# Two MoE expert layouts: narrow column chunks in eleven weight buffers, and rows up to 11 KB in eight

## The chip, the cores and the metric

The kernel runs on one core of a Trainium2 chip. The metric is the device time of one execution in microseconds (us), the median of several runs. The core has five engines: TensorE (PE, matrix products), VectorE (DVE), ScalarE (ACT), GpSimd (POOL), and SyncE (SP), which here issues the transfers of weights from device memory to the on-chip buffer. PE sums into eight accumulator banks.

## The reference, cut to what matters

Two layers of a hybrid block (attention, state space, differential attention) on 256 latent and 256 context tokens of width 1024. The second layer ends with eight SwiGLU experts, of which each latent token uses two:

```python
def _swiglu(h, w_gu, w_down):
    g, u = jnp.split(h @ w_gu, 2, axis=-1)
    return (jax.nn.silu(g) * u) @ w_down

def _moe(h, w_r, b_r, we_gu, we_down):
    ...
    for e in range(N_EXP):
        y = y + gates[..., e:e + 1] * _swiglu(h, we_gu[e], we_down[e])
    return y
```

All is float32. An expert's `w_gu` is 1024 x 5632 (gate columns, then up columns, 2816 each), its `w_down` 2816 x 1024; all eight together are 277 MB, and every one is read once.

## The kernel before

The experts (function `moe`) are the last 700 us or so of the program. The experts are sorted by their number of tokens. Five are computed as **large** ones (`expert`, room for 128 tokens), three as **small** ones (room for 32). The order of the parts is g0, 1, d0, 2, g6, 3, d6, 4, g7, 5, d7: a number alone is a large expert, g a small expert's gate and up (`small_gate_up`), d its down (`small_down`).

*Weight buffers.* `raw_tile` hands out the buffers of a ring in turn, from pools that MRB gives: (5, 1, 5), eleven buffers of 8 KB per partition (1 MB each). SP issues one transfer per buffer, in the order of use, as soon as the buffer's last reader is done. Six of the eleven are free early, before the router has run.

*Large experts.* Tokens are the fixed operand, weights stream through PE. The gate and up columns go in three chunks of 1024, 1024 and 768. For each chunk come the gate's eight steps of 128 rows (two steps per transfer), then the up's eight. In each step (`product`) the weights are split into two parts for full precision: ACT copies a rounded part `mwh` (L1348), DVE subtracts to get the rest `mwl` (L1349; `msplit`, MSB = 4 buffers of each). PE multiplies the tokens' two parts with `mwh` (L1369) and, one step later, the main part with `mwl` (L1358, the correction). After the gate's steps ACT applies silu into `msl` (L1448), after the up's steps DVE multiplies (L1450), PE transposes in blocks of 128 columns (L1455), and ACT and DVE split the transposed block (`mah`, `mal`). Down has 22 steps over the 2816 rows, two per transfer, in the same three passes. The gate's sums lie in two of the three banks S, the up's in the two banks mm, the down's in y and one S.

*Small experts.* 32 tokens fill only a quarter of PE's columns, so four matmuls run in four column groups: two halves of the output columns times two rows of the reduction. Nothing is split; a float32 matmul stands in the profile as two records. Gate and up go in two chunks, 2 x 1024 and 2 x 384 columns, with transfers of [128, 2, 1024] (4 KB pieces of rows) and [128, 4, 384] (1.5 KB pieces). The four partial sums are copied by ACT (L1531) and folded and transposed on PE (`fold`, L1538). The small down has eleven steps, each of one transfer that holds both halves' 128 rows.

*Between the parts* the steps call a generator that gathers the next expert's tokens (transposes and products on PE, copies on ACT and DVE), and each expert's result is scattered into the output rows a little into the next part (`scatter_now`). The order of the instructions on an engine is set when the program is built, by a scheduler that works from the order of the code, and the engine executes them in that order.

Of the kernel before, what the change touches and what calls it, by code (L numbers as in the profile page):

```python
# [12 lines left out]
F = mybir.dt.float32  # L13
# [18 lines left out]
FT = 22  # L32
NE = 8
# [9 lines left out]
XB, START, MRB, MSB = 1, 1, (5, 1, 5), 4  # L43
# [71 lines left out]
def kernel(ctx: ExitStack, tc: tile.TileContext, I, out: bass.AP):  # L115
# [1130 lines left out]
    def moe(L, pp, late, mraw):  # L1246
# [51 lines left out]
        big = mw.tile([128, 6, NE, NE], F, name="big")  # L1298
# [80 lines left out]
        def gather(rk, res, small=False):  # L1379
# [21 lines left out]
            for c in range(2):  # L1401
# [6 lines left out]
                xg = mw.tile([128, 512], F, name="xg", tag="msl", bufs=2)  # L1408
# [19 lines left out]
        def expert(X, gt, gu_src, dn_src, side=()):  # L1428
# [4 lines left out]
            for o, w in ((0, 1024), (1024, 1024), (2048, 768)):  # L1433
                sl = mw.tile([128, 1024], F, name="msl", tag="msl", bufs=2)
                halves = [(c, min(512, w - c)) for c in range(0, w, 512)]
                for a, tag in enumerate(("S", "mm")):
                    pg = [p_(tag, "m" + "gu"[a]) for _ in halves]
                    for kp in range(4):
                        raw = raw_tile([128, 2, w])
                        SP.dma_start(raw, gu_src(kp, a, o, w))  # L1440
# [3 lines left out]
                        if o == 0 and a == 0 and kp == 1:  # L1444
                            scatter_now()
                    for (c, n), p in zip(halves, pg):
                        if a == 0:
                            S.activation(sl[:, c:c + n], p[:, :n], AF.Silu)  # L1448
                        else:
                            V.tensor_tensor(sl[:, c:c + n], sl[:, c:c + n], p[:, :n], op=OP.mult)  # L1450
                for c, n in halves:
                    f = n // 128
# [3 lines left out]
                    ah = mw.tile([128, f, 128], FR, name="mah", tag=f"mah{f}", bufs=5 if f == 4 else 1)  # L1456
                    al = mw.tile([128, f, 128], FR, name="mal", tag=f"mal{f}", bufs=5 if f == 4 else 1)
                    pv = pt[:, :n].rearrange("p (f q) -> p f q", f=f)
# [355 lines left out]
```

## Time and profile before

| | |
|---|---|
| time, median of 3 runs | 1818.12 us (1816.6 to 1825.8) |
| profiled execution, its own time | 1821.04 us |
| its span, first to last instruction | 1819.2 us |
| mean granted clock of PE | 0.951 of full |
| busy share of the span: PE, DVE, ACT | 91%, 63%, 48% |
| chain of work that ended last | PE 77%, DMA 8%, DVE 7% |
| moved by DMA | 436.09 MB |

The profile is of one execution. Its page gives the busy time of each engine, 40 equal slices of the span, the chain of work that ended last, and the costliest groups of instructions; the trace behind it gives any stretch instruction by instruction. The experts stand in slices 25 to 40. In a row of the timeline, x8 is a run of eight records of one line; the end of a matmul is modelled.

### The profile page before, as it was taken

What the parts mean: (1) busy time and instruction counts of PE and PEld (TensorE: products, weight loads), DVE (VectorE), ACT (ScalarE), POOL (GpSimd) and SP (SyncE); (2) the same over time, 40 slices, a digit from 0 to 9 for tenths busy, and PEclk for the clock granted to TensorE, in tenths of its full rate; (3) what the DMA queues carried; (4) which work ended last, traced back from release to release, by engine and by line L of the source; (5) the groups of instructions that cost most, each with busy time, mean ns of one, the idle gap of its engine ahead of it and who ended that gap; (6) DMA issues with size and microseconds to landing.
All of it is one profiled execution on the core that took longest, in us unless ns stands there. A gap on an engine that the chain in (4) does not pass through costs nothing.

```text
span 1819.2 us, 26372 instructions
## 1 busy us (share of the span) xinstructions
PE 1663.7 (91%) x9454; PEld 1244.2 (68%) x9454; DVE 1154.5 (63%) x2224; ACT 874.4 (48%) x1447; POOL 321.9 (18%) x254
## 2 busy tenths in 40 slices
PE   5898989887999999987999984899999999999995
PEld 2677657674988888876786672487686685784782
DVE  4673668658632343288587756288785586982895
ACT  3433545543622132335444652376673574772770
POOL 1221013334420022474232141000000000000000
PEclk8999998878999999999899996899999999999998
DMA  9327454328633233345676227999999999999995
GB/s 306 86 67 236 127 149 123 107 66 269 188 93 96 89 101 96 110 165 167 209 223 207 65 82 300 395 406 409 408 406 376 399 406 409 406 408 387 408 407 229
DMA packets 248153, 436.09 MB, mean 240 GB/s; under 512 B 15025, under 2 KB 166329, under 8 KB 248017
## 3 DMA queue, kind: packets, MB, share of 16 engines
q1 hardware_dynamic: 246096, 429.55, 66.2%
q0 software_dynamic: 1920, 4.81, 1.0%
q8 instruction: 76, 1.25, 0.3%
q14 instruction: 61, 0.49, 0.1%
HBM read 431.08 MB, written 3.23 MB: 239 GB/s over the span
## 4 chain that ended last, share of the span: by engine, by line
PE 77%; DMA 8%; DVE 7%; issue 2%; ACT 2%; POOL 0%; SPq 0%; ACTq 0%; DVEq 0%; POOLq 0%
PE mg L1369 6%; PE mu L1369 6%; PE mdn L1369 5%; PE gu L273 5%; PE gu L274 5%; PE gu L276 4%; DMA raw<-in_w_ada 4%; PE mu L1358 3%; PE mg L1358 3%; PE mdn L1358 3%; PE tok L276 2%; DMA mraw<-in_exp_w_gu 2%; PE ada L316 2%; PE tok L273 2%; PE SC L919 2%; PE tok L274 2%
## 5 line engine op out<-in xcount | busy, mean ns | idle before, releaser
L1349 DVE TENSOR_TENSOR mwl<-mraw,mwh 128x1024 fp32r<-128x1024 f32 (+1 forms) x350 | 389.4, 1160 | 37.2 <-ACT mwh L1348 20.2
L1348 ACT ACTIVATE mwh<-mraw 128x1024 fp32r<-128x1024 f32 (+1 forms) x350 | 337.8, 1013 | 61.4 <-PE mg L1369 22.9
L260 POOL TENSOR_TENSOR wlo<-raw,whi 128x1024 fp32r<-128x1024 f32 (+2 forms) x93 | 224.1, 2416 | 482.2 <-ACT whi L259 435.1
L259 ACT ACTIVATE whi<-raw 128x1024 fp32r<-128x1024 f32 (+2 forms) x168 | 168.2, 1004 | 237.3 <-PE dn L274 71.9
L260 DVE TENSOR_TENSOR wlo<-raw,whi 128x1024 fp32r<-128x1024 f32 (+2 forms) x75 | 90.5, 1206 | 144.1 <-ACT whi L259 142.8
L273 PE MATMUL gu<-HI,whi 128*128 128x512 f32 (+1 forms) x400 | 144.2, 369 | 2.3 <-ACT whi L259 2.3
L274 PE MATMUL gu<-LO,whi 128*128 128x512 f32 (+1 forms) x400 | 144.9, 369 | 0.0
L273 PE MATMUL tok<-whi,HI 128*128 128x256 f32 (+2 forms) x400 | 108.7, 301 | 5.4 <-ACT xin L550 4.3
L274 PE MATMUL tok<-whi,LO 128*128 128x256 f32 (+2 forms) x400 | 106.4, 295 | 5.2 <-DVE LO L444 5.1
L316 PE MATMUL ada<-raw,cT 128*32 128x256 f32 x768 | 75.5, 430 | 37.8 <-DMA raw<-in_w_ada 35.9
L276 PE MATMUL gu<-HI,wlo 128*128 128x512 f32 (+1 forms) x400 | 98.5, 368 | 0.0
L273 PEld LDWEIGHTS tok<-whi,HI 128*128 128x128 f32 x400 | 79.2, 199 | 14.9 <-issue 5.4
L273 PEld LDWEIGHTS gu<-HI,whi 128*128 128x128 f32 x400 | 75.7, 190 | 15.8 <-ACT whi L259 2.5
L274 PEld LDWEIGHTS tok<-whi,LO 128*128 128x128 f32 x400 | 79.3, 199 | 9.1 <-DVE LO L444 5.8
L274 PEld LDWEIGHTS gu<-LO,whi 128*128 128x128 f32 x400 | 76.1, 191 | 12.8
L276 PEld LDWEIGHTS gu<-HI,wlo 128*128 128x128 f32 x400 | 70.5, 189 | 12.9
L273 PE MATMUL dn<-whi,ah 128*128 128x512 f32 x176 | 70.3, 399 | 5.6 <-ACT whi L259 5.6
L276 PE MATMUL tok<-wlo,HI 128*128 128x256 f32 (+2 forms) x400 | 72.3, 299 | 1.9 <-DVE nw L227 1.9
L1369 PE MATMUL mg<-mwh,Xh 128*128 128x512 f32 x240 | 72.5, 383 | 1.7 <-ACT mwh L1348 1.6
L1369 PE MATMUL mdn<-mwh,mah 128*128 128x512 f32 x220 | 70.1, 400 | 0.9 <-ACT mwh L1348 0.9
L1369 PE MATMUL mg<-mwh,Xl 128*128 128x512 f32 x240 | 70.8, 376 | 0.0
L1369 PE MATMUL mu<-mwh,Xl 128*128 128x512 f32 x240 | 70.7, 376 | 0.0
(361 smaller groups left out, 3496.5 us busy)
## 6 DMA issues: line engine op xcount, KB each, us to landing
mraw<-in_exp_w_gu SPq DMA_DIRECT2D x128, 1024.0 KB, 15.8
mraw<-in_exp_w_down SPq DMA_DIRECT2D x88, 1024.0 KB, 15.6
mraw<-in_exp_w_gu SPq DMA_DIRECT2D x64, 768.0 KB, 13.8
raw<-in_w_ada SPq DMA_DIRECT2D x88, 512.0 KB, 4.8
raw<-in_ffn_w_gu SPq DMA_DIRECT2D x100, 256.0 KB, 3.4
raw<-in_w_in SPq DMA_DIRECT2D x38, 512.0 KB, 5.1
raw<-in_ffn_w_down SPq DMA_DIRECT2D x30, 512.0 KB, 3.7
E<-cscr POOLq DMA_DIRECT2D x12, 384.0 KB, 7.2
```

What stands on the lines that cost most here:

```text
L259: S.activation(hi, raw, AF.Copy)
L260: (eng or V).tensor_tensor(lo, raw, hi.bitcast(F), op=OP.subtract)
L273: T.matmul(o, ah, bh, start=start and i == 0, stop=False)
L274: T.matmul(o, *((ah, bl) if wa else (al, bh)), start=False, stop=False)
L276: T.matmul(o, *((al, bh) if wa else (ah, bl)), start=False, stop=stop and i == n - 1)
L316: T.matmul(pa[32 * j:32 * j + 32, hs], cT[:, k], w[j], start=(k == 0), stop=(k == KC - 1), tile_position=(0, 32 * j), skip_group_check=True)
L919: T.matmul(po[:, :n], qTC(t)[b0:b0 + 32, h // 2], kTC[b0:b0 + 32, h // 2, :n], start=True, stop=True)
L1348: S.activation(wh, raw, AF.Copy)
L1349: V.tensor_tensor(wl, raw, wh.bitcast(F), op=OP.subtract)
L1358: T.matmul(pc[:, :w], xh, wl[:, c * 512:c * 512 + w], start=False, stop=stop)
L1369: T.matmul(pc[:, :w], x, wh[:, c * 512:c * 512 + w], start=start and x is xh, stop=False)
```

## The change

- Ring: eleven buffers of 8 KB become eight of 11 KB (MRB = (4, 0, 4)), four of them free early.
- Large gate and up: two chunks of 1408 columns instead of three; a transfer is [128, 2, 1408], pieces of 5.5 KB of a row instead of 4 or 3 KB. Each chunk has three accumulator pieces, 512, 512 and 384: the gate's in S, S, S, the up's in mm, mm and y, the down's in y and mm.
- Small gate and up: one pass over whole rows. A transfer is [128, 2816], one whole row half of 11 KB per partition; two of them make a step.
- Down, large and small: a partition holds two neighbouring rows (8 KB in one piece) instead of two rows that lie 128 apart; the eleventh row of each half comes alone (4 KB). So partition p of a half stands for rows 11p to 11p + 10, and the transposes before down, and the small experts' folds, take every eleventh column of `msl` (`slv`, `views`).
- Split buffers: two of `mwh` and three of `mwl`, 1408 wide, instead of four and four of 1024. `msl` has one buffer of 1408 columns, and the gathered tokens and the results have a pair of buffers of their own.

In all 224 weight transfers instead of 280. The core of the diff:

```diff
-XB, START, MRB, MSB = 1, 1, (5, 1, 5), 4
+XB, START, MRB, MSB = 1, 1, (4, 0, 4), (2, 3)
...
-            wh = ms.tile([128, 1024], FR, name="mwh", tag="mwh", bufs=MSB)[:, :n]
-            wl = ms.tile([128, 1024], FR, name="mwl", tag="mwl", bufs=MSB)[:, :n]
+            wh = ms.tile([128, HW], FR, name="mwh", tag="mwh", bufs=MSB[0])[:, :n]
+            wl = ms.tile([128, HW], FR, name="mwl", tag="mwl", bufs=MSB[1])[:, :n]
...
-            for o, w in ((0, 1024), (1024, 1024), (2048, 768)):
-                sl = mw.tile([128, 1024], F, name="msl", tag="msl", bufs=2)
...
+            for c in range(2):
+                sl = mw.tile([128, HW], F, name="msl", tag="msl", bufs=1)
+                for a, tags in enumerate((("S", "S", "S"), ("mm", "mm", "y"))):
+                    pg = [p_(tag, "m" + "gu"[a]) for tag in tags]
                     for kp in range(4):
-                        raw = raw_tile([128, 2, w])
-                        SP.dma_start(raw, gu_src(kp, a, o, w))
+                        raw = raw_tile([128, 2, HW])
+                        SP.dma_start(raw, gu_src(kp, a, c))
...
+                slv = sl.rearrange("p (q j) -> p j q", j=HB)
+                for b0, f in FOURS:
                     pt = p_tp()
                     for q in range(f):
-                        T.transpose(pt[:, q * 128:(q + 1) * 128], sl[:, c + q * 128:c + (q + 1) * 128], ident)
...
+                        T.transpose(pt[:, q * 128:(q + 1) * 128], slv[:, b0 + q], ident)
...
-            pd = [p_("y", "mdn"), p_("S", "mdn")]
...
+            pd = [p_("y", "mdn"), p_("mm", "mdn")]
+            for c in range(2):
+                for j in range(0, HB, 2):
+                    if c or j:
+                        next(side, None)
+                    n = min(2, HB - j)
+                    raw = raw_tile([128, n, 1024])
+                    SP.dma_start(raw, dn_src(c, j, n))
...
+                    for j in range(2):
+                        raws.append(raw_tile([128, DFF]))
+                        SP.dma_start(raws[j], gu_src(2 * kp + j, a))
...
+                    for (o, n), p in zip(PIECES, pg):
+                        tiles4(lambda h, j, r, tp: T.matmul(
+                            p[r, :n], Xf[:, 2 * kp + j, 0:32], raws[j][:, h * HW + o:h * HW + o + n], start=kp == 0,
+                            stop=kp == 3, tile_position=tp, skip_group_check=True))
...
+            def dn(c, j, n):
+                return rows(WDf, e * DFF + c * HW, HW).rearrange("(p j) n -> p j n", j=HB)[:, j:j + n]
```

The engines' order moves at three places. In the listings a row is a line of the code, the tile written and those read, the shape, in brackets whom it waits for, and xN a repetition. The line numbers of the changed kernel are some 5 higher.

DVE in expert 1, from up to down, before (`msl<-msl,mu` is the product with up, `mal` the rest of a transposed block):

```order
1580 L1450 TENSOR_TENSOR msl<-msl,mu 128x512 [waits PE_49]
1581 L1450 TENSOR_TENSOR msl<-msl,mu 128x256 [waits PE_49]
1582 L1349 TENSOR_TENSOR mwl<-mraw,mwh 128x1024 [waits DMAHW6_49,Activation_49]
1583 L1349 TENSOR_TENSOR mwl<-mraw,mwh 128x1024 [waits Activation_49]
1584 L1460 TENSOR_TENSOR mal<-tp,mah 128x512 [waits Activation_49]
1585 L1460 TENSOR_TENSOR mal<-tp,mah 128x256 [waits Activation_49]
1586 L1349 TENSOR_TENSOR mwl<-mraw,mwh 128x1024 [waits DMAHW7_49,Activation_49]
```

The same place on DVE in the changed kernel:

```order
1564 L1354 TENSOR_TENSOR mwl<-mraw,mwh 128x1024 [waits DMAHW6_49,PE_49,Activation_49]
1565 L1454 TENSOR_TENSOR msl<-msl,mu 128x512 [waits PE_49] x2
1566 L1354 TENSOR_TENSOR mwl<-mraw,mwh 128x1024 [waits Activation_49]
1567 L1454 TENSOR_TENSOR msl<-msl,mu 128x384 [waits PE_49]
1568 L1465 TENSOR_TENSOR mal<-tp,mah 128x512 [waits Activation_49] x2
1569 L1354 TENSOR_TENSOR mwl<-mraw,mwh 128x1024 [waits DMAHW7_49,Activation_49]
1570 L1354 TENSOR_TENSOR mwl<-mraw,mwh 128x1024 [waits PE_49,Activation_49]
1571 L1465 TENSOR_TENSOR mal<-tp,mah 128x384 [waits Activation_49]
```

A split of down's second step now stands between the second and the third product, and the transposed blocks' parts follow later.

PE in g6, where the gate's steps end, before (`mg<-mraw,Xs` is a small expert's gate matmul on one column group):

```order
4898 L1413 MATMUL tp<-cf,xg 128x128 [waits Activation_49]
4899 L1413 MATMUL tp<-cf,xg 128x128 x3
4900 L1524 MATMUL mg<-mraw,Xs 32x512 [waits DMAHW4_49]
4901 L1524 MATMUL mg<-mraw,Xs 32x512 x3
4902 L1524 MATMUL mg<-mraw,Xs 32x512 [waits DMAHW5_49]
4903 L1524 MATMUL mg<-mraw,Xs 32x512 x3
4904 L1524 MATMUL mg<-mraw,Xs 32x512 [waits DMAHW6_49]
4905 L1524 MATMUL mg<-mraw,Xs 32x512 x3
```

PE at the same place of the changed kernel:

```order
4888 L1528 MATMUL mg<-mraw,Xs 32x512 [waits DMAHW7_49]
4889 L1528 MATMUL mg<-mraw,Xs 32x512 x5
4890 L1528 MATMUL mg<-mraw,Xs 32x384 x3
4891 L1528 MATMUL mg<-mraw,Xs 32x512 [waits DMAHW0_49]
4892 L1528 MATMUL mg<-mraw,Xs 32x512
4893 L1528 MATMUL mg<-mraw,Xs 32x384
4894 L1528 MATMUL mg<-mraw,Xs 32x512 [waits DMAHW1_49]
4895 L1528 MATMUL mg<-mraw,Xs 32x512 x5
4896 L1528 MATMUL mg<-mraw,Xs 32x384 x3
4897 L1540 MATMUL tp<-fold,msl 128x64 [waits Activation_49]
4898 L1540 MATMUL tp<-fold,msl 128x64 x3
```

Before, four matmuls follow each transfer, on two column groups. Now three follow the first of two transfers, all on one column group, and nine the second, on the other three; and the folds come when the gate's copies are done, before up.

PE in d0, before (`mdn<-mraw,sact` is a small down's matmul):

```order
4464 L1558 MATMUL mdn<-mraw,sact 32x512 [waits DMAHW4_49]
4465 L1558 MATMUL mdn<-mraw,sact 32x512 x3
4466 L1413 MATMUL tp<-cf,xg 128x128 [waits DVE_49,Activation_49]
4467 L1413 MATMUL tp<-cf,xg 128x128 x3
4468 L1405 MATMUL gather<-tok,Sm 128x512 x4
4469 L1558 MATMUL mdn<-mraw,sact 32x512 [waits DMAHW5_49]
4470 L1558 MATMUL mdn<-mraw,sact 32x512 x3
```

PE at the same place of the changed kernel:

```order
4451 L1564 MATMUL mdn<-mraw,sact 32x512 [waits DMAHW6_49]
4452 L1410 MATMUL gather<-tok,Sm 128x512 [waits DVE_49]
4453 L1410 MATMUL gather<-tok,Sm 128x512 x3
4454 L1418 MATMUL tp<-cf,xg 128x128 [waits Activation_49]
4455 L1418 MATMUL tp<-cf,xg 128x128 x3
4456 L1410 MATMUL gather<-tok,Sm 128x512 x4
4457 L1564 MATMUL mdn<-mraw,sact 32x512 [waits DMAHW7_49]
4458 L1564 MATMUL mdn<-mraw,sact 32x512 x6
```

Before, four matmuls follow one transfer. Now one follows the first of two transfers and seven the second.

## Rows read from the trace of the kernel before

**Rows 1.** Page, slices of the span: DMA busy tenths, GB/s.

```profile
DMA  9327454328633233345676227999999999999995
GB/s 306 86 67 236 127 149 123 107 66 269 188 93 96 89 101 96 110 165 167 209 223 207 65 82 300 395 406 409 408 406 376 399 406 409 406 408 387 408 407 229
```

**Rows 2.** Waits of PE, 1100 to 1800 us: total us, times, longest us.

```profile
PE mu L1524 <- DMA mraw<-in_exp_w_gu: 4.6, 1, 4.6
...
PE mdn L1558 <- DMA mraw<-in_exp_w_down: 1.0, 1, 1.0
```

**Rows 3.** PE's timeline, g6: start us, us, line, operation [idle before it].

```profile
1386.58 0.64 PE L1369 MATMUL mdn<-mwh,mah 128*128 128x512 f32 x2
...
1387.05 0.62 PE L1369 MATMUL mdn<-mwh,mal 128*128 128x512 f32 x2
...
1388.07 1.91 PE L1524 MATMUL mg<-mraw,Xs 128*32 128x512 f32 x8
...
1402.08 3.63 PE L1524 MATMUL mg<-mraw,Xs 128*32 128x512 f32 x24
...
1407.57 7.10 PE L1524 MATMUL mu<-mraw,Xs 128*32 128x512 f32 x64
...
1415.38 2.00 PE L1538 MATMUL tp<-fold,mal 128*128 128x64 f32 x16 [0.72 <-ACT mal L1531]
...
1423.46 3.04 PE L1524 MATMUL mu<-mraw,Xs 128*32 128x384 f32 x28
...
1427.16 0.88 PE L1538 MATMUL tp<-fold,mal 128*128 128x64 f32 x6 [0.65 <-ACT mal L1531]
...
1429.40 0.73 PE L1369 MATMUL mg<-mwh,Xh 128*128 128x512 f32 x2 [1.36 <-ACT mwh L1348]
```

**Rows 4.** SP's timeline in g6; DMA issues, page and 1385 to 1395 us (last: us to landing).

```profile
1390.02 23.84 SPq L1518 DMA_DIRECT2D mraw<-in_exp_w_gu  x13
...
mraw<-in_exp_w_gu SPq DMA_DIRECT2D x128, 1024.0 KB, 15.8
...
mraw<-in_exp_w_gu SPq DMA_DIRECT2D x3, 1024.0 KB, 5.5
```

**Rows 5.** Stretch: us, busy us by engine (records), granted clock, DMA share, GB/s.

```profile
1386.00:1392.00 6.00, 6.00 (x28) 2.45 (x26) 1.46 (x3) 0.83 (x2) 0.00 (x0) 1.00 0.97 341
```

**Rows 6.** Stretches with one row size landing: 3, 4 and 1.5 KB; same columns.

```profile
1209.00:1221.00 12.00, 12.00 (x60) 9.99 (x59) 10.86 (x12) 9.14 (x12) 0.00 (x0) 1.00 1.03 401
1230.00:1280.00 50.00, 48.28 (x234) 33.98 (x233) 37.49 (x41) 28.54 (x33) 0.00 (x0) 1.00 1.03 409
1412.00:1422.00 10.00, 9.28 (x86) 4.52 (x79) 1.33 (x4) 2.95 (x7) 0.00 (x0) 1.00 1.07 373
```

**Rows 7.** Stretch in g0, same columns.

```profile
1150.00:1156.00 6.00, 2.96 (x8) 0.56 (x8) 0.00 (x0) 0.60 (x1) 0.00 (x0) 0.68 1.06 375
```

**Rows 8.** Groups, 1170 to 1290 us, ACT and DVE: busy us, mean ns.

```profile
L1348 ACT ACTIVATE mwh<-mraw 128x1024 fp32r<-128x1024 f32 x59 | 58.9, 1062 | 9.2 <-PE mdn L1369 3.8 <-PE mg L1369 3.4 <-DMA mraw<-in_exp_w_gu 1.3
...
L1448 ACT ACTIVATE msl<-mg 128x512 f32<-128x512 f32 x5 | 2.8, 597 | 5.5 <-PE mg L1358 5.5
...
L1450 DVE TENSOR_TENSOR msl<-msl,mu 128x512 f32<-128x512 f32 x5 | 3.3, 686 | 4.0 <-PE mu L1358 4.0
```

**Rows 9.** PE's timeline, small down d0.

```profile
1266.63 1.06 PE L1558 MATMUL mdn<-mraw,sact 128*32 128x512 f32 x8
...
1280.00 5.36 PE L1558 MATMUL mdn<-mraw,sact 128*32 128x512 f32 x48
```

**Rows 10.** Timeline, expert 1 from up to down, DVE and PE.

```profile
1235.18 1.02 DVE L1450 TENSOR_TENSOR msl<-msl,mu 128x512 f32<-128x512 f32 x2 [1.81 <-PE mu L1358]
...
1236.04 0.82 PE L1455 MATMUL tp<-cf,msl 128*128 128x128 f32 x6
...
1236.12 2.35 DVE L1349 TENSOR_TENSOR mwl<-mraw,mwh 128x1024 fp32r<-128x1024 f32 x2
...
1238.55 0.73 PE L1369 MATMUL mdn<-mwh,mah 128*128 128x512 f32 x2 [0.31 <-ACT mwh L1348]
```

More of the change, by code (lines that the diff above doesn't have):

```diff
@@ L1407, in gather @@
                 yield
-                xg = mw.tile([128, 512], F, name="xg", tag="msl", bufs=2)
+                xg = mw.tile([128, 512], F, name="xg", tag="xg", bufs=2)
                 S.activation(xg, px, AF.Copy)
@@ L1465, in finish_half @@
                 Yl = mw.tile([128, 512], FR, name="Yl", tag="Yl", bufs=2)
[L1466 removed]
+                Y = mw.tile([128, 512], F, name="Y", tag="xg", bufs=2)
                 V.tensor_tensor(Y, p, g2[:, cs_], op=OP.mult)
@@ new lines, in small_gate_up @@
+            act = mw.tile([128, HB, 64], F, name="sact")
+            parts = (mw.tile([128, HW], F, name="msl", tag="msl", bufs=1),
+                     ms.tile([128, HW], F, name="mwl", tag="mwl", bufs=MSB[1]))
+            for a, tags in enumerate((("S", "S", "S"), ("mm", "mm", "y"))):
+                pg = [p_(tag, "m" + "gu"[a]) for tag in tags]
+                for kp in range(4):
+                    raws = []
+                    for j in range(2):
+                        raws.append(raw_tile([128, DFF]))
+                        SP.dma_start(raws[j], gu_src(2 * kp + j, a))
+                    if a or kp > 1:
+                        next(side, None)
+                    for (o, n), p in zip(PIECES, pg):
+                        tiles4(lambda h, j, r, tp: T.matmul(
+                            p[r, :n], Xf[:, 2 * kp + j, 0:32], raws[j][:, h * HW + o:h * HW + o + n], start=kp == 0,
+                            stop=kp == 3, tile_position=tp, skip_group_check=True))
+                    if a == 0 and kp == 1:
+                        scatter_now()
+                for (o, n), p in zip(PIECES, pg):
+                    S.activation(parts[a][:, o:o + n], p[:, :n], AF.Copy)
@@ new lines, in small_gate_up @@
+            views = [t.rearrange("p (q j) -> p j q", j=HB) for t in parts]
+            for b, f in FOURS:
+                pt = p_tp()
+                for a, t in enumerate(views):
+                    for q in range(f):
+                        T.matmul(pt[:, a * 256 + q * 64:a * 256 + (q + 1) * 64], t[:, b + q],
+                                 fold.rearrange("p h s -> p (h s)"), start=True, stop=True)
+                at = act[:, b:b + f]
+                pv = pt.rearrange("p (a f s) -> p a f s", a=2, f=4)[:, :, :f]
+                S.activation(at, pv[:, 0], AF.Silu)
+                V.tensor_tensor(at, at, pv[:, 1], op=OP.mult)
@@ L1549, in small_down @@
             ST = X[2]
[L1550 to L1552 removed]
+            pd = p_("S", "mdn")
+            for j in range(0, HB, 2):
+                if j == 2:
                     scatter_now()
[L1554 removed]
+                if j >= 4:
                     next(side, None)
[L1556 to L1560 removed]
+                    next(side, None)
+                n = min(2, HB - j)
+                raws = []
+                for h in range(2):
+                    raws.append(raw_tile([128, n, 1024]))
+                    SP.dma_start(raws[h], dn_src(h, j, n))
+                for k in range(n):
+                    tiles4(lambda c, h, r, tp: T.matmul(
+                        pd[r], act[:, j + k, 32 * h:32 * h + 32], raws[h][:, k, c * 512:(c + 1) * 512],
+                        start=j + k == 0, stop=j + k == HB - 1, tile_position=tp, skip_group_check=True))
             Y = mw.tile([128, 512], F, name="Yh", tag="Yh", bufs=2)
```

98 lines of the change are left out of this document (20 added, 78 removed).

## The prediction

> **What bounds the kernel now.** I read the page's 40 slices first, then the experts' part alone. From slice 25 on the DMA digits are 9 and the rates stand near 406 GB/s, where they were mostly under 300 earlier [rows 1]: the change works where the transfers never rest. That alone suggests a DMA bound. But the waits of PE (TensorE) between 1100 and 1800 us name a transfer as releaser for only 4.6 us in the first small expert and 1.0 us in the last small down [rows 2]. In between PE goes from work to work. The order of time in a small gate/up (expert g6, 1388.07 to 1429.40 us) shows why both look full: PE has matmuls to the end, and SP issues the last 13 pieces in 23.84 us [rows 3, 4]. So engine and queue are in balance, and the link between them is the ring of weight buffers: when expert 2 ends the rate falls to 341 GB/s [rows 5], and a piece lands 5.5 us after its issue, against 15.8 us over the whole program [rows 4]: the queue has run empty because every slot is full. A faster transfer there finds no slot. The large experts are PE's (it is 12.00 us of 12.00 busy, first of [rows 6]); only the first small expert and the last down wait for data.
>
> The page is of an execution of 1821.0 us (span 1819.2); the median of the three runs is 1818.1, 2.9 less. I sum against 1821.0 and take off 2.9 at the end. About 0.5% (9 us) is what a measurement of this kernel can tell from no change.
>
> **What the transfers save.** Stretches in which pieces of one row size land run at 373 GB/s (1.5 KB rows), 401 (3 KB) and 409 (4 KB) [rows 6]. Per row on one of 16 engines that is 65.9, 122.6 and 160.2 ns: a line of 9.3 ns plus 0.0368 ns per byte. Run on to 5.5, 8 and 11 KB (an estimate) it gives 416, 421 and 425 GB/s. A large gate/up (23.1 MB) falls from 56.7 to 55.5 us, a large down (11.5 MB, last row of each half still 4 KB) from 28.2 to 27.4, a small gate/up from 57.9 to 54.3, a small down by 0.8. That is 5 x 2.0 + 3 x 3.6 + 3 x 0.8 = 23 us of queue time, the most that the change can bring; nothing, if a row beyond 4 KB costs per byte what a 4 KB row does.
>
> How much of it arrives depends on the ring. Eleven slots of 8 KB become eight of 11 KB, 11 MB as before, but an 8 KB piece of down, or the 4 KB piece at the end of a half, also takes a whole slot. The queue's lead at the start of a small gate/up is then 8 x 3.39 = 27.1 us of transfer.
>
> *First small expert (g0).* Its data arrive late: PE waits 4.6 us, the granted clock falls to 0.68 of full, between 2.4 and 1.2 GHz [rows 2, 7]. 3.6 us less transfer, and the last pair of pieces now brings three wide matmuls per column group after it lands: I take -3 (-6 to +2).
>
> *g6 and g7.* Data side: first slots come back 2.4 us in, the queue restarts in some 2 us, the eight remaining pieces take 27.1 and land by 34 to 36 us; one last set of matmuls (2.4), copies (1.8) and 14 folds with a gather (2.9) end at 41 to 43, where before 41.3 passed. PE's side: before, five halves of a step stand alone at 1.91 us (x8), then 3.63, 7.10 and for the 384 columns four runs of 6.9 us together (one of them stands there): 27.2 [rows 3]. From x8, a matmul of 512 columns is 0.92 us on its column group, so one of 384 is 0.69, and a set of three pieces takes 2.4 us. By the new order the gate stands in four lone sets and a run of two, the up in four sets: 10 x 2.4 = 24 us, 3 less. The copies before the folds can't be used piece by piece any more, since a fold takes every eleventh column: 2 waits of 1.7 to 1.9 us for three copies (0.6 us each, [rows 8]) instead of 0.72, 0.65 and 1.36 [rows 3]: +1. Both sides end near 41 to 43: +1 each (-3 to +4).
>
> Those sets rest on a matmul of one column group not blocking the others. The x64 row shows it: the order has four matmuls on groups 0 and 1 before four on 2 and 3, yet 64 records take 7.10 us, eight pairs' worth only if all four groups run together [rows 3]. The Trainium skill ("TensorE: Matmul & The Clock Gate", The mechanism) says that matmuls start and end strictly in the order of the program. By that rule the x64 row would be near 14 us and three matmuls on group 0 would hold up the other nine for 1.84 us. The trace disagrees at the depth of four records on a group that it shows; six in a row, as now, it doesn't show.
>
> *Small downs.* Two pieces now stand for two steps, and the scheduler puts one lone matmul before the second piece and seven behind. Before, five lone steps of 1.06 us and a run of six of 5.36 [rows 9], 10.3 us. Now three lone matmuls (0.98), three groups of seven (two rounds, 1.86) and a run of 5 steps (4.4): 12.9. d0 and d6 +2.6 each (0 to +4); d7 +1.6, as its 1.0 us wait for data goes.
>
> **Large experts: two buffers of split weights instead of four.** A step of 1408 columns is nine matmuls; two of 512 are issued each 0.47 us [rows 3], so 6 x 0.23 + 3 x 0.175 = 1.92 us, and all steps together cost what they did. The split on ACT takes 1.06 us per 1024 columns, so about 1.4 for 1408 [rows 8], and can start when PE is done with the six main matmuls of the step before last. It is ready 1.5 us later; PE needs it after a correction (0.64), the next main pass (1.28) and its correction, 2.56 us later: 1 us of cover, in down 0.7 (1.2 against 0.47 + 0.93 + 0.47). That cover is gone wherever ACT has something else first. Behind the gate three silus (1.7 us) stand before the third split of up: 0.2 us of wait, twice.
>
> The main place is the change from up to down. Before, PE's first product of down uses banks that are long free, and then two transposed blocks that need only the last two products; PE is idle for 0.31 us [rows 10]. Now down's two sums take banks that up has just filled, so the first matmul waits for the first product on DVE (0.69, [rows 8]). The transposes read every eleventh column, so they need all three products, and the order puts a split of 1.2 us (two in 2.35, [rows 10]) before the third: 0.69 + 0.69 + 1.22 + 0.5 = 3.1 us, from which the rest of up's correction and five matmuls of down (1.6 us) are taken: 1.5 to 1.6 us idle in two waits. Then the third split of down stands behind two copies of the transposed blocks (0.6 each): 0.5 us. In sum 2.1 + 0.4 - 0.3 = +2.2; I take 1.8, as a part of the silus' wait is hidden: 5 x 1.8 = +9 (0.5 to 3 each).
>
> The 22 transposes of an expert load weights with a stride of eleven elements; no row of before has a strided weight load. The nearest row is a transpose as it is, six in 0.82 us [rows 10]. Bounds: 0, since the load runs beside other matmuls, and one more transpose of 0.12 us each: 2.7 us per expert, 21 us in all eight. I take 0, the value of those rows.
>
> **Sum:** -3 + 2 x 1 + 2 x 2.6 + 1.6 + 9 = +14.8: 1836 against the profiled execution, 1833 against the median.
>
> **The rivals.**
> (1) *The transfers decide everywhere.* For it: the DMA digits of 9. Against it: the rows on a full ring, and PE's missing waits. If PE's busy time hides waiting, the queue's 23 us arrive, less 2 to 3 for the coarser ends: -20, 1798. Chance 0.12.
> (2) *Gains and losses cancel.* If the scheduler's order meets the chip better than I think, with 0.5 us per large expert, nothing at the small downs and -3 at g0, the sum is about 0 to +2: 1818 to 1820. It decides if the waits at up to down fall below 0.7 us. Chance 0.26.
> (3) *Strided weight loads cost.* At 0.06 to 0.12 us for each of 22 in eight experts, +11 to +21 on my sum: 1844 to 1854. The Trainium skill ("SBUF — State Buffer", Door 1: The DMA port swizzle) says that accesses which leave a 16-byte line each time pay, and allows a stride of 4 fp32 free; here it is 11. No run here shows it yet. Chance 0.13.
> (4) *A column group's three matmuls block the others.* A pair of pieces then costs 3.4 instead of 2.4 us; with six such pairs in g6 and g7 that is +6 each, 1845; g0 hides it behind its data. It decides if six records queued on one group stop the next group's first. Chance 0.09. By the rule of the Trainium skill weighed above ("TensorE: Matmul & The Clock Gate", The mechanism) it would come out so.
> (5) *Rows over 4 KB bring nothing*: g0's gain is gone, g6 and g7 end 3 us later: +9, 1842. Chance 0.06.
> My forecast of 1833 (1825 to 1840) has 0.34.
>
> **How the numbers follow.** Slower by over 0.5% (above 1827): my case without its lowest part 0.31, and rivals 3 to 5 with 0.28: 0.59. Within 0.5%: rival 2 and that lowest part, 0.29. Faster: rival 1, 0.12. For 8 in 10 I leave out most of rival 1 and the upper end of rival 3: 1813 to 1852.
>
> **What would show it.** In the changed profile: landings of gate/up pieces every 3.4 us where the queue is full, rates of 415 to 425 GB/s there, and more stretches below 380 at the ends of large experts, since the ring fills sooner. PE's waits should name DVE's product (msl) and ACT's split (mwh) at up to down, about 2 us per large expert, and a wait of some 1.8 us for the copies before folds. The large experts should grow by about 2 us each, the small downs by 2 to 3. I am wrong if those parts shrink (rival 1), if transposes take visibly more than 0.14 us each (rival 3), or if up's four steps in g6 take 14 instead of 10 us (rival 4).

## The result, and the profile after

The changed kernel takes 1870.12 us, median of four runs (1866.5 to 1875.6); the kernel before took 1821.47 beside it. The ratio is 1.027, with a 95% interval of 1.0228 to 1.0313: slower by 49 us, and beyond the upper end of the predicted range (1852). The profiled execution took 1872.4 us (span 1870.7), mean granted clock 0.947.

I compare by parts, from a part's first matmul to that of the next. In the profile after, g0 begins 6.3 us earlier (1120.1 against 1126.4 us); in all the profiles below it begins between 1117 and 1132, and I leave that aside. Each small part is taken with the large expert behind it, because the scheduler lets neighbours overlap by a few matmuls. Lengths in us, of one profile each; the ratios are of medians against the kernel before on the same chip. A part's first matmul doesn't cut the work at the same place in every kernel, as the last matmuls of the large expert before can follow it: at g6 2 records in the kernel before and in b4_ring8, 14 in the changed kernel, e2_folds, e9_olddown, b3_split23 and b5_both, 20 in e5_oldsmall. Two records take 0.47 us, so up to 4 us stand one column further right. At d7 they are 20 in the changed kernel and 2 before: some 4 of the 6.5 us by which d7 grows.

| kernel | g0+1 | d0+2 | g6+3 | d6+4 | g7+5 | d7 | ratio (95%) |
|---|---|---|---|---|---|---|---|
| before | 140.3 | 121.4 | 136.2 | 121.1 | 135.9 | 38.0 | 1 |
| after | 145.6 | 129.3 | 152.6 | 125.7 | 152.8 | 44.5 | 1.027 (1.0228 to 1.0313) |
| e1_order | 146.0 | 128.0 | 155.8 | 129.6 | 149.7 | 42.4 | 1.0343 (1.0318 to 1.0367) |
| e2_folds | 142.3 | 127.5 | 146.7 | 124.2 | 146.4 | 40.7 | 1.0188 (1.0166 to 1.021) |
| e7_rows | 142.8 | 126.6 | 145.2 | 123.2 | 145.2 | 38.8 | 1.0144 (1.0107 to 1.0181) |
| e4_order_folds | 143.1 | 127.1 | 146.2 | 127.5 | 147.2 | 41.0 | 1.0203 (1.0163 to 1.0243) |
| e5_oldsmall | 145.9 | 120.3 | 151.5 | 120.6 | 153.5 | 40.1 | 1.0241 (1.0223 to 1.0259) |
| e9_olddown | 147.8 | 119.5 | 152.6 | 119.9 | 152.4 | 36.6 | 1.0203 (1.0168 to 1.0239) |
| b5_both | 145.0 | 118.5 | 148.2 | 117.1 | 148.9 | 37.8 | 1.0113 (1.0074 to 1.0152) |
| b4_ring8 | 142.2 | 121.1 | 143.7 | 121.2 | 146.1 | 36.8 | 1.0108 (1.004 to 1.0175) |
| b3_split23 | 138.3 | 118.5 | 140.4 | 118.5 | 141.2 | 36.8 | 1.004 (1.0012 to 1.0068) |

Of the 58 us by which the parts grow, 33 stand at g6 with 3 and g7 with 5 (the whole profile grows by 51.5, since g0 begins earlier). The slices of the page (after) show what became of the queue that never rested:

```profile
DMA  9227354249432333446682359979989979989975
GB/s 306 80 79 231 104 161 150 57 149 269 125 101 91 101 93 100 153 153 221 193 249 61 109 214 421 416 278 369 413 321 421 415 288 376 414 330 420 402 274 217
```

Against [rows 1] the peaks are higher, 413 to 421 instead of 406 to 409, and there are holes of 278 to 330 where there were none. The transfers did become faster, and between them the queue stood still. PE's waits of the changed kernel, 1100 to 1820 us (total us, times, longest us), answer to [rows 2]:

```profile
PE mu L1528 <- DMA mraw<-in_exp_w_gu: 5.3, 7, 1.0
PE tp L1460 <- DVE msl L1454: 3.6, 5, 0.7
...
PE mdn L1374 <- DVE msl L1454: 2.3, 5, 0.5
PE tp L1540 <- ACT mwl L1534: 1.9, 3, 0.6
```

Transfers are named for 5.3 us only. PE's timeline of g6 after (start us, us, line, operation [idle before it]), beside [rows 3]:

```profile
1394.98 2.55 PE L1528 MATMUL mg<-mraw,Xs 128*32 128x512 f32 x6
...
1400.91 3.45 PE L1528 MATMUL mg<-mraw,Xs 128*32 128x512 f32 x24
...
1419.88 4.21 PE L1540 MATMUL tp<-fold,msl 128*128 128x64 f32 x16 [0.62 <-ACT msl L1534]
1424.03 9.90 PE L1528 MATMUL mu<-mraw,Xs 128*32 128x512 f32 x72
1434.76 2.55 PE L1528 MATMUL mu<-mraw,Xs 128*32 128x512 f32 x6 [0.83 <-DMA mraw<-in_exp_w_gu]
1438.16 2.56 PE L1528 MATMUL mu<-mraw,Xs 128*32 128x512 f32 x18 [0.85 <-DMA mraw<-in_exp_w_gu]
1441.35 4.21 PE L1540 MATMUL tp<-fold,mwl 128*128 128x64 f32 x16 [0.62 <-ACT mwl L1534]
1445.35 1.68 PE L1540 MATMUL tp<-fold,msl 128*128 128x64 f32 x6
1446.83 1.69 PE L1540 MATMUL tp<-fold,mwl 128*128 128x64 f32 x6
1448.28 2.06 PE L1410 MATMUL gather<-tok,Sm 128*128 128x512 f32 x4
1450.13 1.38 PE L1374 MATMUL mg<-mwh,Xh 128*128 128x512 f32 x3
```

Three things are to be seen. Sixteen records of folds take 4.21 us where they took 2.00. A pair of pieces takes 3.45 us alone and 3.3 in a run of three, where I had 2.4. And at the end everything is twice as long, the next expert's matmuls too (1.38 against 0.80 us a few rows later): the granted clock has fallen to 1.2 GHz. Which of these carries the loss, the rows don't tell, since PE looks busy under each.

### The profile page after: what moved, and what is told of

Read it like the earlier page. It is cut to its first block, busy times and chain, and to the rows that moved or that the text cites. A ratio compares the mean times of both kernels' runs of the same rounds, so it can differ in the third digit from the quotient of the medians.

```text
span 1870.7 us, 25886 instructions
## 1 busy us (share of the span) xinstructions
PE 1709.1 (91%) x9454; PEld 1284.5 (69%) x9454; DVE 1153.1 (62%) x2144; ACT 871.6 (47%) x1367; POOL 323.1 (17%) x254
## 5 line engine op out<-in xcount | busy, mean ns | idle before, releaser
L1354 DVE TENSOR_TENSOR mwl<-mraw,mwh 128x1408 fp32r<-128x1408 f32 (+1 forms) x270 | 391.4, 1461 | 102.4 <-ACT mwh L1353 100.0
L1353 ACT ACTIVATE mwh<-mraw 128x1408 fp32r<-128x1408 f32 (+1 forms) x270 | 336.7, 1256 | 130.9 <-PE mg L1374 54.4
L265 DVE TENSOR_TENSOR wlo<-raw,whi 128x1024 fp32r<-128x1024 f32 (+2 forms) x75 | 90.5, 1207 | 146.2 <-ACT whi L264 145.2
L281 PEld LDWEIGHTS gu<-HI,wlo 128*128 128x128 f32 x400 | 70.5, 189 | 12.9
L1374 PE MATMUL mg<-mwh,Xh 128*128 128x512 f32 (+1 forms) x240 | 72.1, 412 | 1.8 <-ACT Xh L1422 1.8
L1374 PE MATMUL mdn<-mwh,mal 128*128 128x512 f32 x220 | 70.5, 394 | 0.0
L279 PE MATMUL dn<-whi,al 128*128 128x512 f32 x176 | 70.0, 398 | 0.0
```

What stands on the lines that cost most here:

```text
L265: (eng or V).tensor_tensor(lo, raw, hi.bitcast(F), op=OP.subtract)
L279: T.matmul(o, *((ah, bl) if wa else (al, bh)), start=False, stop=False)
L281: T.matmul(o, *((al, bh) if wa else (ah, bl)), start=False, stop=stop and i == n - 1)
L1374: T.matmul(pc[:, :w], x, wh[:, c * 512:c * 512 + w], start=start and x is xh, stop=False)
```

## The experiments

**First set: what PE does in the small experts.** e1_order undoes the blocking by the order alone:

```diff
-                    for (o, n), p in zip(PIECES, pg):
+                    with tc.manual_schedule(engines={mybir.EngineType.PE}):
+                        for (o, n), p in zip(PIECES, pg):  # and tiles4 takes j = 1 before j = 0
```

> The changed kernel, and only the order of a small expert's gate/up matmuls on PE is set by hand: the first matmul of a pair of pieces is one that reads the later piece, and the twelve go piece by piece over the four column groups. Theory ORDER (three matmuls on one column group hold up the other nine): a pair in a run falls from 3.3 to 2.4 us and one that waits for data from 5.1 to 2.5, g6 and g7 fall by 6 us each, d7's and g0's neighbours not at all: 1870 falls to 1856. Theory FOLDS (the strided weight loads of the folds, 0.26 us each, and the clock that falls behind them carry the loss): g6 and g7 stay above 52 us, 1866 to 1872.

Measured: 1878.52 us (1873.1 to 1884.8), no gain, and above both lines. The edit does what it should: a pair takes 2.57 us. But PE then waits 25.3 us for transfers instead of 5.3, and its clock falls. Waits and timeline of g6 in e1_order, and one stretch (us, busy us by engine (records), granted clock, DMA share, GB/s):

```profile
PE mu L1529 <- DMA mraw<-in_exp_w_gu: 25.3, 9, 4.2
...
1401.42 2.57 PE L1529 MATMUL mg<-mraw,Xs 128*32 128x512 f32 x24
...
1426.45 4.92 PE L1529 MATMUL mu<-mraw,Xs 128*32 128x512 f32 x24 [4.21 <-DMA mraw<-in_exp_w_gu]
1433.23 4.92 PE L1529 MATMUL mu<-mraw,Xs 128*32 128x512 f32 x24 [1.86 <-DMA mraw<-in_exp_w_gu]
...
1416.00:1442.00 26.00, 16.29 (x92) 5.36 (x85) 3.16 (x2) 4.50 (x6) 0.00 (x0) 0.68 1.01 419
```

So the matmuls of g6 can't end before its last pieces land. The slow order had only filled that time; the wait of 5.3 us in the profile hid a bound by data.

e2_folds takes the stride out of the folds, e3_transp out of the large experts' transposes:

```diff
-                        T.matmul(pt[...], t[:, b + q],          # t: every eleventh column
+                        T.matmul(pt[...], t[:, (HB - 1 - b - q) * 128:(HB - b - q) * 128],
```

```diff
-                        T.transpose(pt[...], slv[:, b0 + q], ident)
+                        T.transpose(pt[...], sl[:, (HB - 1 - b0 - q) * 128:(HB - b0 - q) * 128], ident)
```

> The changed kernel, and the folds of the small experts read 128 neighbouring columns instead of every eleventh (the last block first, so that they still wait for all three copies); the permutation of down's rows is thereby left out in the small experts. Theory FOLDS: a fold takes 0.13 instead of 0.26 us, 22 of them 2.8 us less in each of three experts, the granted clock stays at 1.00 behind them where it was 0.50 for up to 10 us, another 3 us each: 1870 falls to 1853 (1850 to 1858). Theory ORDER: the folds' 0.26 us come from the clock, which falls for another reason, and the stride costs nothing: 1868 to 1872, folds at 0.13 us only where the clock is 1.00.

> The changed kernel, and only the transposes of the large experts read 128 neighbouring columns instead of every eleventh (the last block first, so that they wait for the same products); the permutation of down's rows is thereby left out in the large experts. Theory: these transposes run among other matmuls, 290 against 272 ns each in the two traces, and the large experts have time to spare against the queue: 5 x 22 x 0.02 = 2 us, 1866 to 1870. Rival (strided loads cost 0.13 us each as in the folds): 14 us, 1856.

Measured: e2_folds 1853.40 us (1849.3 to 1855.8), 17 less than the changed kernel (15 by the ratios), as expected; e3_transp 1869.54 (1865.6 to 1879.1), no difference that shows. The groups of weight loads (PEld) and of the transposes' matmuls (line, operation, count | busy us, mean ns of one), first of the changed kernel, then of e2_folds, then of e3_transp:

```profile
L1540 PEld LDWEIGHTS tp<-fold,mwl 128*128 128x128 f32 x66 | 16.8, 345 | 4.0 <-ACT mwl L1534 4.0
L1460 PEld LDWEIGHTS tp<-cf,msl 128*128 128x128 f32 x110 | 15.5, 210 | 7.2 <-DVE msl L1454 5.7 <-DVE mal L1465 1.0
L1460 PE MATMUL tp<-cf,msl 128*128 128x128 f32 x110 | 17.2, 290 | 3.6 <-DVE msl L1454 3.6
```

```profile
L1540 PEld LDWEIGHTS tp<-fold,mwl 128*128 128x128 f32 x66 | 7.8, 192 | 2.3 <-ACT mwl L1534 2.3
```

```profile
L1460 PEld LDWEIGHTS tp<-cf,msl 128*128 128x128 f32 x110 | 12.5, 141 | 7.8 <-DVE msl L1454 5.7 <-DVE mal L1465 1.3
L1460 PE MATMUL tp<-cf,msl 128*128 128x128 f32 x110 | 15.7, 277 | 3.5 <-DVE msl L1454 3.5
```

A load of every eleventh column costs more in both places, 345 against 192 ns and 210 against 141. In the transposes, whose matmul has 128 columns, the matmuls grow only from 277 to 290 ns, 1.5 us in all 110. A fold has a matmul of only 64 columns, and there the loads set the pace; why a transpose's load loses less, the rows don't say. The stretches show the folds, of the changed kernel (in the first, PEld is busy 1.00 of 1.00 us at full clock) and of e2_folds:

```profile
1420.00:1421.00 1.00, 1.00 (x5) 1.00 (x5) 0.00 (x0) 0.00 (x0) 0.00 (x0) 1.00 0.91 383
...
1443.00:1453.00 10.00, 10.00 (x35) 9.13 (x35) 4.66 (x7) 4.52 (x7) 0.00 (x0) 0.52 1.02 417
```

```profile
1442.00:1444.00 2.00, 1.96 (x17) 1.83 (x17) 0.77 (x2) 1.59 (x3) 0.00 (x0) 1.00 1.01 414
1444.00:1446.00 2.00, 2.00 (x10) 1.65 (x10) 1.91 (x2) 2.00 (x4) 0.00 (x0) 1.00 1.03 420
```

With the stride the clock falls during the folds and stays near 0.5 for ten us, into expert 3; without it, it stays at 1.00. The pace of the folds themselves is the same at either level: twelve records take 2.93 us from 1445.35 us on, at 0.50, and sixteen 4.15 from 1419.88 on, mostly at 1.00. What the low clock slows is the work behind them. The end of g6 in e2_folds, which begins at 1394.51 us:

```profile
1437.75 2.56 PE L1528 MATMUL mu<-mraw,Xs 128*32 128x512 f32 x18 [0.86 <-DMA mraw<-in_exp_w_gu]
...
1444.77 0.80 PE L1374 MATMUL mg<-mwh,Xh 128*128 128x512 f32 x3
```

The last matmuls of up start 43.2 us behind g6's first matmul, to the tenth as in the changed kernel; what is left until expert 3 takes 7.0 us instead of 12.0. So the stride, with the clock that it lowers, costs 5 us in g6, and all of them behind the last data. The Trainium skill ("SBUF — State Buffer", Door 1: The DMA port swizzle) has a penalty for accesses that change the 16-byte line each time; the loads here agree in direction, with the numbers above.

e4_order_folds has both edits of e1_order and e2_folds.

> Both edits of the two kernels before: order of the small gate/up's matmuls by hand, folds from neighbouring columns (the permutation of down's rows left out in the small experts). If the two costs lie one behind the other, the gains add: 1870 falls to 1839 (1834 to 1845). If one hides behind the other, because both only fill a wait for the same transfers, it is no better than the better of the two: 1852 to 1857.

Measured: 1858.74 us (1848.4 to 1863.3), no better than e2_folds alone. The order hides behind the data: PE waits 26.7 us for transfers here. The folds that come after the last data don't.

**Second set: why the data are late.** e5_oldsmall keeps the changed kernel and puts `small_gate_up`, `small_down` and their sources back as they were.

> The changed kernel's ring, large experts and down with two rows per partition there, but the small experts as in the kernel before (two column chunks, pieces of 8 and 6 KB, now each in an 11 KB slot of eight). Theory that the small experts' new code carries the loss: g0, g6, g7, d0, d6, d7 go back to 45, 41, 41, 21, 21, 38 us, the large ones keep what they had beyond the clock, +2 each: 1870 falls to 1830 (1826 to 1835). Rival RING (eight slots instead of eleven carry it): 8 MB of lead instead of 11, so g6 and g7 stay about 7 us longer than before, and d0 and d6 2 us: 1845 to 1850.

Measured: 1861.96 us (1860.1 to 1864.0). Both lines were too low. The old small code in the new buffers is only 8 us better than the new code (5 by the ratios), and g6 stands at 53.9 us with it. What differs is what has landed when g6 begins. From g6's first matmul to the end, 173.0 MB of weights are used (two gate/ups of 23.07 MB, two small downs of 11.53, three experts of 34.60). What the DMA still moves in that time, of before, after and b5_both:

```profile
DMA packets 49621, 165.18 MB, mean 383 GB/s; under 512 B 2712, under 2 KB 10904, under 8 KB 49586
```

```profile
DMA packets 26346, 169.77 MB, mean 357 GB/s; under 512 B 2249, under 2 KB 2249, under 8 KB 16329
```

```profile
DMA packets 50769, 169.59 MB, mean 375 GB/s; under 512 B 2784, under 2 KB 10976, under 8 KB 50734
```

About 2.5 MB of it are other transfers (results, norms, instructions). So 10.3 MB had landed before, and 5.7 in the changed kernel. I call this the lead. SP's issues agree with it: the first piece of g6 is issued 30.9 us ahead of g6's first matmul in the kernel before (at 1357.22 us), and 15.2 us ahead in the changed one (at 1379.81), where SP waits for buffers that DVE's splits of expert 2 still read. Three kernels take it away from the kernel before, piece by piece:

```diff
-XB, START, MRB, MSB = 1, 1, (5, 1, 5), 4
+XB, START, MRB, MSB = 1, 1, (5, 1, 5), (2, 3)     # b3_split23
+XB, START, MRB, MSB = 1, 1, (4, 0, 4), (4, 4)     # b4_ring8
+XB, START, MRB, MSB = 1, 1, (4, 0, 4), (2, 3)     # b5_both
```

> The kernel before with two buffers of mwh and three of mwl instead of four and four; its ring of eleven, its pieces and its small experts stay. Theory LEAD (a small gate/up, 23.1 MB, lives on the megabytes that have landed when it starts: 10.3 MB before g6 in the kernel before, 5.7 MB in the changed one; half of the loss comes from splits that can't run ahead, so that the raw buffers are held until PE is nearly there): the lead at g6 falls by two pieces to 8 MB, g6 and g7 grow by 5 us each, 1818 goes to 1832 (1825 to 1840). Rival SLOTS (the number of buffers in the ring alone makes the lead): under 3 us, 1818 to 1822.

> The kernel before with a ring of eight 8 KB buffers instead of eleven; four and four split buffers, its pieces and its small experts stay. Theory LEAD in either form: three pieces of 1.05 MB less, 7.7 us of transfer at 409 GB/s, the lead at g6 falls from 10.3 to 7.2 MB, g6 and g7 grow by 7 us each and d0, d6 by 1: 1818 goes to 1834 (1830 to 1840). Theory CODE (e5 lost through the large experts' 1408-wide chunks, not the ring): the queue still fills what PE needs, 1818 to 1823.

> The kernel before with both: a ring of eight 8 KB buffers, two of mwh and three of mwl. Theory LEAD: the two losses add, the lead at g6 is 4.5 to 5 MB as in e5_oldsmall (4.4), g6 and g7 stand at 53 to 55 us: 1818 goes to 1852 (1845 to 1862), most of what e5 lost (1862). Theory CODE: the wide chunks of the large experts are needed for the loss, and this one stays below 1835.

Measured: b3_split23 1826.01 us (ratio 1.004), b4_ring8 1844.10 (1.0108), b5_both 1841.11 (1.0113, runs from 1832 to 1857), which lies between its two lines. The same code of g6 takes longer with less lead:

| | before | b3_split23 | b4_ring8 | b5_both | e5_oldsmall |
|---|---|---|---|---|---|
| landed at g6's start, MB | 10.3 | 8.7 | 7.7 | 5.9 | 4.4 |
| length of g6, us | 41.3 | 43.0 | 48.9 | 51.9 | 53.9 |

Only b4_ring8 begins g6 at the same point of the work as the kernel before. Between these two it is 7.6 us for 2.6 MB, 2.9 us per MB; at the 368 GB/s of g6 in b4_ring8 a MB needs 2.7 us. (Some 1.2 of the 7.6 us come from a lower clock: up's last twelve records take 2.74 us there and 1.49 in b5_both.) In b3_split23 and b5_both twelve more records of expert 2 stand behind g6's first matmul, in e5_oldsmall eighteen: g6 begins some 2.8 and 4.2 us earlier, is that much longer, and has less landed by then. The changed kernel's 5.7 MB are read 2.8 us early in the same way. That is also why d0+2 and d6+4 are 3 to 4 us shorter in b5_both than in b4_ring8. So the five columns are no scale of us per MB, but the direction holds. The buffers cost about 21 us of the 49 (13 to 28 by the interval of b5_both). The two losses don't add as I expected: the short ring alone makes 20 of it, and fewer splits on top of it nothing that shows. At the end of g6 in b5_both PE waits for each piece:

```profile
1432.80 1.49 PE L1524 MATMUL mu<-mraw,Xs 128*32 128x384 f32 x12 [0.43 <-DMA mraw<-in_exp_w_gu]
1434.93 0.84 PE L1524 MATMUL mu<-mraw,Xs 128*32 128x384 f32 x4 [0.64 <-DMA mraw<-in_exp_w_gu]
1437.03 1.49 PE L1524 MATMUL mu<-mraw,Xs 128*32 128x384 f32 x12 [1.26 <-DMA mraw<-in_exp_w_gu]
```

**Third set: the other pieces.** e9_olddown is e5_oldsmall with the old down in the large experts as well, so the wide gate/up and the buffers alone are left; e7_rows is the changed kernel with rows 128 apart everywhere:

```diff
-                return rows(WDf, ...).rearrange("(p j) n -> p j n", j=HB)[:, j:j + n]
+                return rows(WDf, ...).rearrange("(j p) n -> p j n", p=128)[:, j:j + n]   # e7_rows, and reads of neighbouring columns
```

> e5_oldsmall, and the large experts' down as in the kernel before too: eleven transfers of two rows 128 apart instead of twelve, two of which are half full, and transposes of neighbouring columns. What is left of the change are the 1408-wide gate/up of the large experts and the buffers. b5_both, with old code throughout and as few buffers, took 1841, e5_oldsmall 1862. Theory ODD (the half-full pieces and 11 KB buffers for 8 KB pieces cost lead): the lead at g6 rises from 4.4 to 5.5 MB, g6 and g7 fall by 2.5 us each and the other parts by 1 each: 1862 falls to 1850 (1845 to 1855). Rival WIDE (the wide pieces are held longer and cost the lead): 1858 to 1864.

> The changed kernel without the permutation of down's rows: a partition holds rows 128 apart again (4 KB pieces of a row in the same transfers of two rows and one), and transposes and folds read neighbouring columns. Everything is computed. Theory: it gains what e2_folds gained, since the queue rests in the large experts and 4 KB pieces cost nothing there, and the first folds can start a copy earlier: 1870 falls to 1851 (1847 to 1855). Rival (the 8 KB pieces of down are worth their 409 to 421 GB/s): 92 MB of down cost 6 us more, 1857 to 1860.

Measured: e9_olddown 1856.20 us (1854.0 to 1858.4), between its two lines; e7_rows 1847.11 (1842.6 to 1852.0), as its theory had it. That makes a ladder by the ratios of the medians. Each ratio is known to some 7 us, so a step to some 10:

- buffers alone +21 (b5_both);
- the wide large gate/up in 11 KB buffers, with one `msl` buffer and accumulators in other banks, +16 more (e9_olddown). This is not the lead at g6, which is 6.0 MB in e9_olddown and 5.9 in b5_both; what it is stays open;
- the small experts' whole rows without any stride, and down in twelve pieces, -11 (e7_rows). Faster transfers are a likely reason, but the order of the matmuls, the copies and the pieces of down change too, and I didn't separate them;
- the two neighbouring rows with their strides, +23 (the changed kernel). Of these the folds' stride is 15 to 17 (e2_folds). The rest may be the copies and products that the strided reads must all wait for; that I didn't separate.

**Fourth set: data or PE, in the changed kernel itself.** a7_ring7 takes one buffer away (`MRB = (4, 0, 3)`); a8_less and b7_less leave out the last loads of up:

```diff
-                    raws = []
+                    if a == 0 or kp < 3:        # else the two pieces before are read again
+                        raws = [raw_tile([128, DFF]) for j in range(2)]
```

> The changed kernel with seven 11 KB buffers instead of eight, nothing else. Theory LEAD: a piece of 1.44 MB less has landed when g6 and g7 start (4.3 instead of 5.7 MB), 3.4 us each at 422 GB/s, and as much at most at g0: 1870 goes to 1878 (1875 to 1882). Theory PE (the folds and the order of the matmuls alone make the loss in g6 and g7): 1868 to 1872.

> The changed kernel, and the last two pieces of a small expert's up (2.88 MB) are not loaded: its last matmuls read the two pieces before once more. This leaves out a part of the weights; PE's work is the same. Theory LEAD (g6 and g7 are bound by 17.4 MB that have still to come): 6.8 us less in each of g6 and g7, up to as much in g0: 1870 falls to 1853 (1849 to 1858). Theory PE: 1867 to 1872.

> The same in the kernel before: the last two 1.05 MB pieces of the first column chunk of a small expert's up are not loaded, the two pieces before are read once more, PE's work is the same. Theory LEAD: 10.3 MB have landed when g6 starts, so g6 itself doesn't wait, but queue and PE are in balance over g6 and expert 3 together; of 5.2 us of transfer per small expert a third at most arrives: 1813 to 1819. Rival (before is bound by the queue as the changed kernel is): 5 us each, 1804 to 1808.

Measured: a7_ring7 1881.96 us (1871.5 to 1882.9), 12 more, at the upper end of what LEAD expected; a8_less 1861.09 (1857.8 to 1862.1), 9 less, half of what LEAD expected; b7_less 1811.24 (ratio 0.9963), between its two lines. By parts a8_less gains only 3.2 us at g6+3 and 3.4 at g7+5, where 6.8 each were expected, and the rest mostly in the small downs and their neighbours. In a8_less up's four pairs run through without a wait in 12.19 us, where they took 16.7 with the waits. So the changed kernel's g6 has two bounds close together: take the data's lateness away, and the order of the matmuls and the folds are next; take the order away, and the data are next. The kernel before is bound by data in g0 only: b7_less shortens g0+1 by 5.7 us and nothing else by more than 1.4.

**A version that beats both.** b1_order is the kernel before with its small gate/up in an order set by hand; b6_ring12_order adds a twelfth buffer (`MRB, MSB = (5, 2, 5), (3, 3)`).

> The kernel before, and only the order of its small gate/up matmuls set by hand: the first of a step reads the later of the two pieces, so that no step stands as two lone halves. Theory LEAD (g and the large expert behind it are bound by the queue together): g6 and g7 fall by 3 to 4 us each, experts 3 and 5 grow by as much, 1815 to 1821. Rival PE: the gain stays, 1810 to 1814.

> The kernel before with a ring of twelve 8 KB buffers, paid for by three and three split buffers, and the order of the small gate/up's matmuls set by hand. Theory LEAD: one more piece, 1.05 MB, less half a piece for the splits: g6 with expert 3 and g7 with expert 5 fall by 1 to 3 us each, and with more in hand the faster order pays: 1820 falls to 1813 (1808 to 1819). Rival: the ring is long enough at eleven, 1817 to 1822.

Measured: b1_order 1823.63 us (ratio 1.0022, 1.0002 to 1.0042), just above both lines; b6_ring12_order 1812.79 (0.9963, 0.9943 to 0.9983): faster than before by 0.4%, as LEAD had it. The lead at g6 is 11.0 MB there, and g6+3 takes 133.6 us instead of 136.2. The order alone gains nothing; whether the buffer alone would, without the order and the three and three splits, I didn't run.

## Why the prediction was wrong

Two terms of the sum failed: the strided weight loads, put at 0, and the lead, read from the ring's size. Both can be read off g6. I had its last pieces landing 34 to 36 us behind its first matmul and 7.1 us of work behind them; they land at 43 (some 40 counted from where the kernel before begins g6), and the work takes 12.0. The waits for the copies before the folds, 1.8 us each in my sum, came to 0.6.

**The strided weight loads** were taken as 0, with 0.12 us per load as the other end, because "the load runs beside other matmuls". For the transposes, whose row it was taken from, 0 is close (1.5 us in all). It was carried over to the folds, where the loads set the pace. A fold is two records of 0.26 instead of 0.13 us, so 22 folds cost about 6 us more per small expert, past the upper bound of 2.7. The clock that falls behind them slows the next expert's start. In g0 with 1, which grew by 5.3 us where I had a gain of 1.2, the stride is 3.3 (e2_folds). Rival 3 was this mechanism, with too small a chance, because I had put folds and transposes under one row. That its price of 11 to 21 us fits the 15 to 17 measured is partly luck: it spread one load per fold and transpose over eight experts, and nearly all of the cost lies in the folds of three.

**The lead was read from the ring's size.** The step "The queue's lead at the start of a small gate/up is then 8 x 3.39 = 27.1 us of transfer" took the ring as full of g6's pieces. It held 5.7 MB, 13.5 us at 421 GB/s, so 17.4 MB, 41 us, had still to come. Pieces of expert 2's down still fill buffers until shortly before g6, and SP waits for them. I should have measured the lead of the kernel before, 10.3 MB, from the trace, and then asked what each buffer that goes is worth. The change took buffers away in both rings, and my sum has no term for it but 1 us of cover at the splits. b5_both puts that missing term at 21 us, the largest part of the miss.

**Rival 4, the blocking**, did happen, at a smaller price: three matmuls of one group take 2.55 us alone, and a lone pair 3.45, where 2.57 is possible (e1_order). But in a run the second pair adds only 2.4 us (two take 5.81 us in e2_folds at full clock), so about 0.9 us are lost per run, and not per pair. The 3.3 us per pair in the run of three above have the fallen clock in them. The rule of the Trainium skill ("TensorE: Matmul & The Clock Gate", The mechanism), that matmuls start in the order of the program, agrees with this depth of six records. And without the loss PE waits for data (e1_order, e4_order_folds). My set of 2.4 us was itself a little low: 0.92 + 0.92 + 0.69 is 2.5.

**The large experts** were right in the place and some two thirds of the size. Up to down in expert 1 after, beside [rows 10]:

```profile
1234.61 1.29 DVE L1454 TENSOR_TENSOR msl<-msl,mu 128x512 f32<-128x512 f32 x2 [0.47 <-PE mu L1363]
1235.44 0.47 PE L1374 MATMUL mdn<-mwh,mah 128*128 128x512 f32 x1 [0.46 <-DVE msl L1454]
...
1237.55 1.24 PE L1460 MATMUL tp<-cf,msl 128*128 128x128 f32 x8 [0.72 <-DVE msl L1454]
```

Both waits are there, at the places named, 1.2 us together where I had 1.5 to 1.6; 5.9 us in the five experts. The waits for ACT's splits, 0.4 and 0.5 us in each, are not in the list of waits. In their place PE waits 1.8 us each for the gathered tokens at the start of experts 1 and 5, which I had not foreseen. The five parts 1 to 5 of e9_olddown against b5_both sum to 492.5 against 483.5 us: +9.0, my number, but not my mechanism. The transposes of e9_olddown read neighbouring columns, and its waits for `msl` come to 1.8 us in all.

**The small downs** were right in the matmuls: seven groups in d0 take 13.4 us (12.9 predicted). Rows of d0 after, beside [rows 9]:

```profile
1265.72 1.04 PE L1564 MATMUL mdn<-mraw,sact 128*32 128x512 f32 x2
...
1269.68 1.92 PE L1564 MATMUL mdn<-mraw,sact 128*32 128x512 f32 x14
...
1285.44 4.50 PE L1564 MATMUL mdn<-mraw,sact 128*32 128x512 f32 x40
...
1290.77 4.82 PE L1577 MATMUL scat<-Yh,ST 64*128 64x512 f32 x8 [0.83 <-DVE Yh L1570]
...
1296.00:1298.00 2.00, 2.00 (x6) 1.61 (x6) 1.86 (x2) 0.00 (x0) 0.00 (x0) 0.50 1.03 422
```

What was not foreseen is behind them. The scheduler now puts all eight records of the scatter in one run ahead of expert 2, where four stood before and the others lay between its steps; and the granted clock is 0.50 from 1294 to 1300 us (last row, a stretch of expert 2's start). d0+2 grew by 7.9 us where I had 4.4, with expert 2's 1.8. I made no experiment on this place.

**The transfers** had the right rate: 421 GB/s over all of g6, and in e4_order_folds, where every pair of up waits for its data, the pairs start 6.8 us apart, 3.4 us per piece. What the faster rows were worth by themselves no run shows; e7_rows is 11 us below e9_olddown, with other changes in it. In the large experts they had little to give, as the queue stood still at times: the holes of 278 to 330 GB/s.

## What to carry to other kernels

A ring of buffers is worth the bytes that have landed when the hungry stage begins, not its size: measure them from the trace, and price every buffer that a change takes away at its bytes over the queue's rate, as a first estimate. Before the lengths of a part are compared, see that its first instruction cuts the work at the same place. A wait that the profile does not show may be filled by slow work; before a slow order is blamed, ask when the data for the next step land. A duration taken from a row holds only where the same things run beside it: a weight load beside a matmul of 128 columns says nothing of one beside 64.

## What the runs showed of the hardware

Weight loads of every eleventh float32 column took 345 ns where neighbouring columns took 192 (folds), and 210 against 141 (transposes). In a row of strided folds a record starts every 0.24 to 0.26 us, at a granted clock of 1.00 as at 0.50. In and behind a run of such folds, in which the weight loads were busy all the time, the granted clock fell from 1.00 to 0.50; it stayed there for about three us at g6's first run and for about ten at its second. With neighbouring columns it stayed at 1.00 in the same place. In e1_order it fell to 0.50 while PE waited 4.2 us between two pairs, and pairs then took 4.92 instead of 2.57 us: the faster order made its own next steps slower.
